# Full-width weights for the narrow value passes: zero columns in the coefficient tiles, and one more key block split, in a two-layer decoder trunk

## The chip, the cores and the metric

The kernel is one program on one core of a Trainium2 chip. The metric is device microseconds for one execution, as the median of the runs of a kernel. The engines are named as in the profile: PE is TensorE's matrix multiply, PEld its weight load, DVE is VectorE, ACT is ScalarE, POOL is GpSimd, SP is SyncE, which issues the large loads.

## The reference

256 tokens of width 1024 go through two layers. Each layer mixes tokens (an mLSTM in the first, an RG-LRU in the second, cross attention beside both), normalises, and then sends every token through 8 heads of 16 experts out of 16384 (PEER). The change lies in that last step:

```python
def block(xb):                       # for the tokens of one group
    q = (xb @ w_q).reshape(n, PEER_HEADS, 2, PEER_HALF)
    s = einsum('nhpc,pkc->nhpk', q, sk)
    sv, si = lax.top_k(s, PEER_TOPK)
    cand = sv[:, :, 0, :, None] + sv[:, :, 1, None, :]
    ...
    fv, fi = lax.top_k(cand, PEER_TOPK)
    gw = softmax(fv)
    act = gelu(einsum('nhkd,nd->nhk', u_tab[eid], xb))
    return einsum('nhk,nhkd->nd', gw * act, v_tab[eid])
...
x = layer_norm(DN_ALPHA * x + mix, ln1_g[i], ln1_b[i])
y = peer_ffn(x, peer_w_q[i], peer_subkeys[i], peer_u[i], peer_v[i])
x = layer_norm(DN_ALPHA * x + y, ln2_g[i], ln2_b[i])
```

Everything is float32.

## The kernel before

A layer runs in stages, one after the other: input projection, token mixer and cross attention, output projection, normalisation, PEER. Products of float32 matrices are mostly made of two parts each: a value is rounded to a shorter format (the high part, `H`), and what is left over is the low part (`L`); high by high, high by low and low by high are added up in PSUM.

PEER does not gather experts for the first 192 tokens. It treats the 16384 experts as 128 blocks of 128 and multiplies all of them:

- **Key stage.** For each key block, `u_step` (L1276) forms 128 experts by 192 tokens. A block is split into `wH` and `wL` and takes 8 pairs of matmuls (L1289, L1290), and one matmul later, the fold (L1299), which adds the tokens' low part; or it is "plain": the raw float32 block is multiplied in 8 calls of `fp32` (L306), which the trace shows as 16 matmuls, and nothing is split. `way` (L53) says which: of the first ten blocks, 3 and 7 are plain and the others are `POOLED`, that is, GpSimd makes their low part; some of the later ones are plain, the others are split on ACT and DVE. Beside this stage VectorE picks the top experts of each token (L1109 to L1117, with the scores `s` from L306), and then the dense gates.
- **Value stage.** For each of the 128 value blocks, the raw block is cast to `wH` on ACT (L146), the low part `wL` is `raw - wH` on DVE (L161), and the coefficients of the block go into a tile `cc`, 128 experts by 512 columns: ACT copies the 192 tokens' high part (L1524) and once more that of tokens 128 to 191 (L1525), DVE subtracts the low part (L1526). `coef` does this two blocks ahead.
- **The last 64 tokens** have their experts gathered row by row (POOL L1226), with a dot product (DVE L1246) and a weighted sum (DVE L1250) for each row. `deal` hands these out between the blocks, at rates from a table.

PE's work for one value block is ten matmuls of 512 streamed columns, weights from `cc`, streams from `wH` and `wL`: two at L1543 (`second`: low and high parts of tokens 128 to 191, 64 columns each, against `wH`, for each half of the model width), then L1552, L1553, L1552, L1553 and twice L1550 (`first`: tokens 0 to 127, high by high, low by high, high by low), then two at L1541 (`second` with `low`: high part of tokens 128 to 191 against `wL`). The last one has only 64 columns of weights, and only 64 partitions of its bank are written:

```python
mm(y[2 + k][:N - P], cc[:, P:N], l[:, ks], start=False, stop=False, ...)
```

Of `cc`, columns 0 to 191 hold the high parts of all tokens, 192 to 383 the low parts, and 384 to 447 again the high parts of tokens 128 to 191; 448 to 511 are not used. The tiles rotate through a pool of three buffers. In the first layer the last 3 blocks, in the second the last 7, are kept, and what is left of their passes comes after the loop in another order; the second layer has tiles of its own for their coefficients.

What sets the order: each engine runs its instructions in the order of the program. `pump` and `load` (L123 to L181) issue the load of a raw block on SP as soon as one of five raw buffers comes free; there are three buffers for `wH` and `wL`. `self.pool_cols` says how many columns of a low part go to GpSimd and how many to VectorE for a block of kind `None`; it is set to 1024 after the first half of the query projection and to 0 in `route`.

Of the kernel before, what the change touches and what calls it, by code (L numbers as in the profile page):

```python
# [7 lines left out]
F32 = mybir.dt.float32  # L8
F32R = mybir.dt.float32r
# [9 lines left out]
P = 128  # L19
# [34 lines left out]
def way(i):  # L54
    if i >= P - 1:
        return PLAIN
    if i >= N0:
        return PLAIN if i - N0 < STEPS and (i - N0) % 12 not in (1, 4, 6, 9, 11) else None
    if i < 10:
        return PLAIN if i % 4 == 3 else POOLED  # L60
    if i < 15:
        return PLAIN
    return PLAIN if i < 44 and i % 5 in (1, 3) else None
# [24 lines left out]
class Trunk:  # L88
# [1239 lines left out]
    def peer_layer(self, layer):  # L1328
        nc, tc, A = self.nc, self.tc, self.A
        self.layer = layer  # L1330
        with ExitStack() as ctx:
# [29 lines left out]
            with ExitStack() as rctx:  # L1361
# [23 lines left out]
                def route():  # L1385
                    for q in range(2):
                        self.score(qT, sk, ss[1], 1, q)
                    yield 0.1
                    yield from self.keys16(w, 1, ss[1], range(2))
                    for q in range(2):  # L1390
                        self.score(qT, sk, ss[0], 0, q)
                    yield from self.keys16(w, 1, ss[1], range(2, 4))
                    rest = self.keys16(w, 0, ss[0], range(4))
                    for c in rest:
                        yield c
                        if self.n_got >= self.u0[layer] + 2:
                            break
                    while self.n_got < self.u0[layer] + 2:
                        yield None
                    for q in range(2, 4):  # L1400
                        self.score(qT, sk, ss[1], 1, q)
                    for _ in range(2):
                        c = next(rest, None)
                        if c:
                            yield c
                    self.pool_cols = 0
                    yield from self.keys16(w, 1, ss[1], range(4, 8))
                    for q in range(2, 4):
                        self.score(qT, sk, ss[0], 0, q)
                    yield from self.routing(w, 1)  # L1410
                    first, n = self.ready, 0
                    for side in (rest, self.keys16(w, 0, ss[0], range(4, 8)), self.routing(w, 0)):
                        for c in side:
                            yield c
                            n += 1
                            if n == LATE:
                                first()
                                self.listed = True
                                yield 2.2
                    for _ in range(LATE):  # L1420
                        yield None
                    self.ready()
# [35 lines left out]
                for gq in range(2):  # L1458
                    qb = self.proj_t(8, (self.xH, self.xL))
                    for b in range(4):  # L1460
                        o = 8 * gq + 2 * b
                        put = (nc.scalar.copy, nc.vector.tensor_copy)[b % 2]
                        put(qT[:, o:o + 2, :].rearrange("p a b -> p (a b)"), qb[b])
                    if gq == 0:
                        def wait():
                            self.pool_cols = D
                            yield
                            yield from paced()
                        self.beside(wait())
# [47 lines left out]
            kept = HL_BUFS - 1  # L1517
            block = lambda i: lo[:, i, :] if i < N0 else hi[:, i - N0, :]

            kept, ccs = KEPT[layer], []  # L1520

            def coef(i):
                cc = ccs[i - P] if layer and i >= P - kept else cp.tile([P, 512], F32R, name="cc")
                nc.scalar.copy(cc[:, :N], block(i))  # L1524
                nc.scalar.copy(cc[:, 2 * N:3 * N - P], block(i)[:, P:])  # L1525
                nc.vector.tensor_sub(cc[:, N:2 * N], block(i), cc[:, :N].bitcast(F32))  # L1526
                return cc
            cs = [coef(0), coef(1)]
            g.append((self.u_step(), None))
# [7 lines left out]
            def second(part, k, low=False):  # L1537
                ks = slice(512 * k, 512 * k + 512)
                for i_, (h, l), cc in part:
                    if low:  # L1540
                        mm(y[2 + k][:N - P], cc[:, P:N], l[:, ks], start=False, stop=False, skip_group_check=True)  # L1541
                    else:
                        mm(y[2 + k], cc[:, N + P:N + 2 * P], h[:, ks], start=i_ == 0, stop=False, skip_group_check=True)  # L1543

            def first(part, c0, n, low=False):
                k, cs_ = c0 // 512, slice(c0, c0 + n)
                out = y[k][:, c0 - 512 * k:c0 - 512 * k + n]
                for i_, (h, l), cc in part:
                    if low:
                        mm(out, cc[:, :P], l[:, cs_], start=False, stop=False, skip_group_check=True)  # L1550
                    else:
                        mm(out, cc[:, :P], h[:, cs_], start=i_ == 0, stop=False, skip_group_check=True)  # L1552
                        mm(out, cc[:, N:N + P], h[:, cs_], start=False, stop=False, skip_group_check=True)  # L1553

            def lead(i):
                return min(HL_BUFS + max(0, min(kept - HL_BUFS, (i - RISE) // 3)), P - i)
            for i in range(P):
                late.append((i, self.next(lead(i)), cs.pop(0)))
                if layer and i == N0:
                    lo_p.close()  # L1560
                    t = right.enter_context(tc.tile_pool(name="tail1", bufs=1, side="right"))
                    self.extra = [[t.tile([P, D], F32R, name=f"v{z}{c}") for z in "HL"] for c in range(kept - HL_BUFS)]
                    ccs += [t.tile([P, 512], F32R, name=f"cc{c}") for c in range(kept)]
                    t.tile([P, 8], F32, name="gap")
                if i + 2 == CLOSES[layer]:
                    for _ in few:
                        pass
                    nc.sync.dma_start(last[1][P - NS:], last[0][:NS])
                    if layer == 0:
                        right.close()  # L1570
                        kv = self.later.enter_context(tc.tile_pool(name="kv1", bufs=1, side="right"))
                        self.memctx = self.later.enter_context(ExitStack())
                        m = self.memctx.enter_context(tc.tile_pool(name="mem1", bufs=1, side="right"))
                        self.wb = kv.tile([P, 28, P], F32, name="wb")
                        self.mem_dest(kv, m)
                        self.lncol = m.tile([P, 5, 2, DT], F32, name="lncol")[:, 0]
                        nc.sync.dma_start(self.lncol, A["ln_col"])
                        self.kvw = [(m.tile([P, D], F32R, name=f"kH{c}"), m.tile([P, D], F32R, name=f"kL{c}"))
                                    for c in range(3)]
                        self.part_v = m.tile([P, 512], F32, name="half")  # L1580
                if i + 2 < P:
                    cs.append(coef(i + 2))
                if layer == 0 and i == MEM1[0]:
                    nc.sync.dma_start(self.part_v, self.half_v)
                if i > 1:
                    self.deal(few, RATES[3][layer])
                if 0 <= i - JOIN[layer] < 4:
                    z, k = divmod(i - JOIN[layer], 2)
                    rs, ks = slice(P - NS, P), slice(512 * k, 512 * k + 512)
                    xs = x[rs, 1, ks]  # L1590
                    nc.vector.scalar_tensor_tensor(xs, xs, 1.0 if z else ALPHA, last[z][rs, ks], op0=ALU.mult, op1=ALU.add)
                if i < P - HALVED[layer]:
                    second(late[-1:], 0), second(late[-1:], 1)
                    first(late[-1:], 0, 512)
                    if i < P - kept:
                        first(late[-1:], 512, 512)
                        first(late[-1:], 512, 512, True)
                    first(late[-1:], 0, 512, True)
                    second(late[-1:], 0, True), second(late[-1:], 1, True)
                    if i < P - kept:  # L1600
                        late.pop()
# [24 lines left out]
            for low in (False, True):  # L1626
                for i_, (h, l), cc in late:
# [2 lines left out]
                        mm(out, cc[:, :P], l[:, ks], start=False, stop=False, skip_group_check=True)  # L1630
                    else:
                        mm(out, cc[:, :P], h[:, ks], start=i_ == late[0][0], stop=False, skip_group_check=True)
                        mm(out, cc[:, N:N + P], h[:, ks], start=False, stop=False, skip_group_check=True)
            if layer:
                for _ in self.norm(y, True, False):
                    pass
# [161 lines left out]
```

## Time and profile before

| | us |
|---|---|
| median of 3 runs | 1627.72 (1627.47 to 1627.94) |
| the profiled execution | 1626.55 |
| its span, first to last instruction | 1624.8 |
| PE busy in the span | 1610.8 (99%) |
| DVE busy | 1444.5 (89%) |
| ACT busy | 1012.3 (62%) |
| POOL busy | 519.5 (32%) |
| value stage of layer 0, first matmul | at 531.81 |
| value stage of layer 1, first matmul | at 1321.63 |

The granted clock of PE is 0.998 in the mean. A row of a timeline gives the start of a matmul, its duration, the line, the tiles, the size of its weights and its output. Matmuls are pipelined: a row's duration of some 390 ns is longer than the distance to the next row's start, so what a matmul costs is read from the distances between starts and not from durations.

### The profile page before, as it was taken

What the parts mean: (1) busy time and instruction counts of PE and PEld (TensorE: products, weight loads), DVE (VectorE), ACT (ScalarE), POOL (GpSimd) and SP (SyncE); (2) the same over time, 40 slices, a digit from 0 to 9 for tenths busy, and PEclk for the clock granted to TensorE, in tenths of its full rate; (3) what the DMA queues carried; (4) which work ended last, traced back from release to release, by engine and by line L of the source; (5) the groups of instructions that cost most, each with busy time, mean ns of one, the idle gap of its engine ahead of it and who ended that gap; (6) DMA issues with size and microseconds to landing.
All of it is one profiled execution on the core that took longest, in us unless ns stands there. A gap on an engine that the chain in (4) does not pass through costs nothing. (4 is left out here: it accounts for less than half of the span.)

```text
span 1624.8 us, 29358 instructions
## 1 busy us (share of the span) xinstructions
PE 1610.8 (99%) x10175; PEld 1454.6 (90%) x10175; DVE 1444.5 (89%) x2921; ACT 1012.3 (62%) x2281; POOL 519.5 (32%) x369
## 2 busy tenths in 40 slices
PE   9999999999999999999999999999999999999998
PEld 9999999999999777777789799999999987777776
DVE  6677899989999899998879989999999988989987
ACT  6554444567776666666768544445787766666664
POOL 3005623443224334331100164245222333343300
PEclk9999999999999999999999999999999999999999
DMA  7656759998889999999756375999888899999983
GB/s 254 210 178 227 245 208 332 334 349 296 288 298 356 335 356 361 351 352 302 269 201 201 100 260 195 327 308 365 313 283 298 315 346 352 345 354 343 351 289 135
DMA packets 133924, 470.42 MB, mean 290 GB/s; under 512 B 15116, under 2 KB 18960, under 8 KB 133520
## 3 DMA queue, kind: packets, MB, share of 16 engines
q1 hardware_dynamic: 94984, 330.64, 58.3%
q0 software_dynamic: 36864, 134.23, 22.6%
q10 hardware_dynamic: 1928, 3.67, 0.6%
q8 instruction: 81, 1.33, 0.3%
q14 instruction: 67, 0.55, 0.1%
HBM read 465.47 MB, written 1.31 MB: 287 GB/s over the span
## 5 line engine op out<-in xcount | busy, mean ns | idle before, releaser
L146 ACT CAST wH<-raw 128x1024 fp32r<-128x1024 f32 (+3 forms) x488 | 501.0, 1028 | 326.4 <-PE bank L1553 173.4
L161 DVE TENSOR_TENSOR wL<-raw,wH 128x1024 fp32r<-128x1024 f32 (+3 forms) x452 | 540.3, 1197 | 105.5 <-ACT wH L146 90.2
L1289 PE MATMUL bank<-xHL,wH 128*128 128x384 f32 x1280 | 378.7, 362 | 0.0
L1290 PE MATMUL bank<-xHL,wL 128*128 128x192 f32 x1280 | 320.3, 250 | 0.0
L1226 POOL DMA_INDIRECT row<-in_v_dram,lot x128 | 211.9, 1656 | 337.7 <-DVE rep L1250 292.4
L1226 POOL DMA_INDIRECT row<-in_u_rows_dram,lot x128 | 177.7, 1388 | 356.4 <-DVE sums L1246 183.7
L306 PE MATMUL bank<-xF,raw 128*128 128x192 f32 x1536 | 267.2, 328 | 0.0
L306 PEld LDWEIGHTS bank<-xF,raw 128*128 128x128 f32 x1536 | 247.4, 190 | 0.0
L1290 PEld LDWEIGHTS bank<-xHL,wL 128*128 128x128 f32 x1280 | 244.4, 191 | 0.0
L1289 PEld LDWEIGHTS bank<-xHL,wH 128*128 128x128 f32 x1280 | 240.5, 188 | 0.0
L1552 PE MATMUL bank<-wH,cc 128*128 128x512 f32 x488 | 192.5, 395 | 0.0
L1553 PE MATMUL bank<-wH,cc 128*128 128x512 f32 x488 | 190.1, 390 | 0.0
L1250 DVE SCALAR_TENSOR_TENSOR rep<-row,coefs,rep 128x1024 f32<-128x1024 f32 x124 | 158.4, 1278 | 0.0
L1246 DVE CUSTOM_DVE_ANT_0 row<-row,rep 128x1024 f32<-128x1024 f32 x128 | 155.9, 1218 | 0.4 <-DMA row<-in_u_rows_dram,lot 0.2
L1541 PE MATMUL bank<-wL,cc 128*64 128x512 f32 x488 | 153.1, 394 | 0.0
L1543 PE MATMUL bank<-wH,cc 128*128 128x512 f32 x488 | 151.5, 391 | 0.0
L1550 PE MATMUL bank<-wL,cc 128*128 128x512 f32 x488 | 149.8, 387 | 0.0
L159 POOL TENSOR_TENSOR wL<-raw,wH 128x1024 fp32r<-128x1024 f32 (+1 forms) x46 | 95.3, 2076 | 141.1 <-DVE x L355 87.4
L235 PE MATMUL bank<-xHL,wL 128*128 128x256 f32 x488 | 136.2, 279 | 1.3 <-POOL wL L151 0.6
L233 PE MATMUL bank<-xHL,wH 128*128 128x256 f32 x488 | 136.9, 280 | 0.4 <-ACT xHL L498 0.4
L234 PE MATMUL bank<-xHL,wH 128*128 128x256 f32 x488 | 135.7, 278 | 0.9 <-DVE xHL L502 0.7
L1274 ACT ACTIVATE oh<-oh,gL 128x128 f16<-128x128 f16 x384 | 125.8, 434 | 8.3 <-DVE oh L1268 8.2
(379 smaller groups left out, 2733.0 us busy)
## 6 DMA issues: line engine op xcount, KB each, us to landing
raw<-in_v_dram SPq DMA_DIRECT2D x256, 512.0 KB
raw<-in_u_dram SPq DMA_DIRECT2D x242, 512.0 KB
raw<-in_w_q_dram SPq DMA_DIRECT2D x32, 512.0 KB
raw<-in_w_out_dram SPq DMA_DIRECT2D x16, 512.0 KB
wglo<-in_u_dram SPq DMA_DIRECT2D x14, 512.0 KB
raw<-in_w0qx_dram SPq DMA_DIRECT2D x8, 512.0 KB
raw<-in_w0v_dram SPq DMA_DIRECT2D x8, 384.0 KB
raw<-in_w0o_dram SPq DMA_DIRECT2D x8, 384.0 KB
```

The source lines that it names most:

```text
L146: (nc.vector.tensor_copy if self.cast_dve else nc.scalar.copy)(h[:, c], r[:, c])
L161: rest = lambda l=l, r=r, h=h, c=slice(k, n): nc.vector.tensor_sub(l[:, c], r[:, c], h[:, c].bitcast(F32))
L306: self.nc.tensor.matmul(out, lhsT, rhs, start=start, stop=stop, skip_group_check=True)
L1226: self.nc.gpsimd.indirect_dma_start(to, None, rows, bass.IndirectOffsetOnAxis(ap=self.lot[:, 0, n:n + 1].bitcast(I32), axis=0))
L1246: nc.vector.tensor_tensor_reduce(r, r, rep, 1.0, 0.0, ALU.mult, ALU.add, sums[:, n:n + 1])
L1250: nc.vector.scalar_tensor_tensor(acc[0] if n == NS - 1 else rep, r, c, rep, op0=ALU.mult, op1=ALU.add)
L1289: mm(two(g[:, :2 * N]), h[:, c], two(self.xHL[:, dt, :])[:, :, :N], start=dt == 0, stop=False, skip_group_check=True)
L1290: mm(g[:, :N], l[:, c], self.xH[:, dt, :N], start=False, stop=False, skip_group_check=True)
L1541: mm(y[2 + k][:N - P], cc[:, P:N], l[:, ks], start=False, stop=False, skip_group_check=True)
L1543: mm(y[2 + k], cc[:, N + P:N + 2 * P], h[:, ks], start=i_ == 0, stop=False, skip_group_check=True)
L1552: mm(out, cc[:, :P], h[:, cs_], start=i_ == 0, stop=False, skip_group_check=True)
L1553: mm(out, cc[:, N:N + P], h[:, cs_], start=False, stop=False, skip_group_check=True)
```

## The change

The diff does four things.

1. Of the first ten key blocks of each layer, block 3 is no longer plain. It is of kind `None`: cast on ACT (L146), low part on VectorE (L161), two-part matmuls and a fold. Block 7 stays plain.
2. `self.pool_cols = 0` moves from `route` to the end of the second half of the query projection, which comes earlier.
3. The coefficient tiles are three fixed tiles, taken in turn, in place of a pool that rotates. Columns 192 to 255 of each are set to zero once, by a multiplication of 64 columns of the identity by 0 (`blank`); the seven tiles of the second layer's last blocks are treated likewise when they are made, at value block 64. The low part of the coefficients moves from column 192 to column 256, the second copy of the high part from 384 to 448.
4. The last pass of each block (L1541 before, L1548 after) has 128 columns of weights, 64 of coefficients and 64 of zeros, and writes all 128 partitions of its bank; to the lower half it adds zeros.

```diff
-        return PLAIN if i % 4 == 3 else POOLED
+        return {3: None, 7: PLAIN}.get(i, POOLED)
...
-                    self.pool_cols = 0
...
-                    if gq == 0:
+                    if gq:
+                        self.pool_cols = 0
+                    else:
...
-            kept, ccs = KEPT[layer], []
+            kept, LOW = KEPT[layer], 2 * P
+
+            def blank(cc):
+                nc.vector.tensor_scalar(cc[:, N:LOW], self.ident[:, :LOW - N], 0.0, None, op0=ALU.mult)
+                return cc
+            ring = [blank(cp.tile([P, 512], F32R, name=f"cc{k}", bufs=1)) for k in range(HL_BUFS)]
+            ccs = {}
...
-                cc = ccs[i - P] if layer and i >= P - kept else cp.tile([P, 512], F32R, name="cc")
+                cc = ccs.get(i, ring[i % HL_BUFS])
                 nc.scalar.copy(cc[:, :N], block(i))
-                nc.scalar.copy(cc[:, 2 * N:3 * N - P], block(i)[:, P:])
-                nc.vector.tensor_sub(cc[:, N:2 * N], block(i), cc[:, :N].bitcast(F32))
+                nc.scalar.copy(cc[:, LOW + N:], block(i)[:, P:])
+                nc.vector.tensor_sub(cc[:, LOW:LOW + N], block(i), cc[:, :N].bitcast(F32))
...
-                        mm(y[2 + k][:N - P], cc[:, P:N], l[:, ks], start=False, stop=False, skip_group_check=True)
+                        mm(y[2 + k], cc[:, P:LOW], l[:, ks], start=False, stop=False, skip_group_check=True)
                     else:
-                        mm(y[2 + k], cc[:, N + P:N + 2 * P], h[:, ks], start=i_ == 0, stop=False, skip_group_check=True)
+                        mm(y[2 + k], cc[:, LOW + P:], h[:, ks], start=i_ == 0, stop=False, skip_group_check=True)
...
-                        mm(out, cc[:, N:N + P], h[:, cs_], start=False, stop=False, skip_group_check=True)
+                        mm(out, cc[:, LOW:LOW + P], h[:, cs_], start=False, stop=False, skip_group_check=True)
...
-                    ccs += [t.tile([P, 512], F32R, name=f"cc{c}") for c in range(kept)]
+                    for c in range(kept):
+                        ccs[P - kept + c] = blank(t.tile([P, 512], F32R, name=f"late{c}"))
```

Three places show what this does to the order of the instructions.

PE, in the middle of layer 0's value stage, one block before the change (`cc` is the coefficient tile, the sizes are those of the output):

```order
L1543 MATMUL bank<-wH,cc 128x512 x2
L1552 MATMUL bank<-wH,cc 128x512
L1553 MATMUL bank<-wH,cc 128x512
L1552 MATMUL bank<-wH,cc 128x512
L1553 MATMUL bank<-wH,cc 128x512
L1550 MATMUL bank<-wL,cc 128x512 x2
L1541 MATMUL bank<-wL,cc 64x512 x2
```

and one after it (`cc_6537` is one of the three fixed tiles):

```order
L1550 MATMUL bank<-wH,cc_6537 128x512 x2
L1559 MATMUL bank<-wH,cc_6537 128x512
L1560 MATMUL bank<-wH,cc_6537 128x512
L1559 MATMUL bank<-wH,cc_6537 128x512
L1560 MATMUL bank<-wH,cc_6537 128x512
L1557 MATMUL bank<-wL,cc_6537 128x512 x2
L1548 MATMUL bank<-wL,cc_6537 128x512 x2
```

The ten matmuls stand in the same order; the last two write 128 partitions in place of 64, and the line numbers are 7 higher.

DVE, at the start of layer 0's value stage (`wglo` and `wghi` are the coefficients of the first and second half of the blocks; L1524 after is `blank`, L1533 after the low part of L1526 before), a piece of the difference:

```order
 L161 TENSOR_TENSOR wL<-raw,wH 128x1024
 L1326 TENSOR_TENSOR wghi<-wghi,bank 128x192
-L1526 TENSOR_TENSOR cc<-wglo,cc 128x192 x2
+L1524 TENSOR_SCALAR cc_6537<-ident 128x64
+L1524 TENSOR_SCALAR cc_6539<-ident 128x64
+L1524 TENSOR_SCALAR cc_6541<-ident 128x64
+L1533 TENSOR_TENSOR cc_6537<-wglo,cc_6537 128x192
+L1533 TENSOR_TENSOR cc_6539<-wglo,cc_6539 128x192
 L161 TENSOR_TENSOR wL<-raw,wH 128x1024
```

Three operations of 64 columns come ahead of the coefficients of the first two blocks; everything else keeps its place.

DVE, early in layer 0's key stage, after the query projection (`s` are the scores, `sv` and `sidx` the top values and their places, `qT` the queries):

```order
 L1111 MAX_INDEX sidx_1659<-sv_1657,s_1663 128x8 x2
 L1113 MATCH_REPLACE tmp<-sv_1657,s_1663 128x128 x2
-L1463 COPY qT<-bank 128x512 x2
+L1462 COPY qT<-bank 128x512 x2
 L1115 MAX sv_1657<-tmp 128x8 x2
 L1117 MAX_INDEX sidx_1659<-sv_1657,tmp 128x8 x2
+L161 TENSOR_TENSOR wL<-raw,wH 128x1024
 L1109 MAX sv_1658<-s_1664 128x8 x2
 L1111 MAX_INDEX sidx_1660<-sv_1658,s_1664 128x8 x2
```

The low part of key block 3 is one more VectorE operation, just ahead of the first maximum of the next scores. On ACT the cast of this block and the copy for its fold are added; on PE its 8 plain matmuls give way to pairs of L1289 and L1290, with the fold after the next block has begun. In layer 1 the same happens at the same places, and seven more `blank` operations stand at value block 64. POOL and SP issue the same instructions in the same order.

More of the change, by code (lines that the diff above doesn't have):

```diff
@@ L1632, in peer_layer @@
                         mm(out, cc[:, :P], h[:, ks], start=i_ == late[0][0], stop=False, skip_group_check=True)
-                        mm(out, cc[:, N:N + P], h[:, ks], start=False, stop=False, skip_group_check=True)
+                        mm(out, cc[:, LOW:LOW + P], h[:, ks], start=False, stop=False, skip_group_check=True)
             if layer:
```

## The prediction

> **What bounds the kernel now.** I read the page's busy line first, then the table of stretches, then PE's timeline in the value stage, then its groups by shape.
>
> ```profile
> PE 1610.8 (99%) x10175; PEld 1454.6 (90%) x10175; DVE 1444.5 (89%) x2921; ACT 1012.3 (62%) x2281; POOL 519.5 (32%) x369
> GB/s 254 210 178 227 245 208 332 334 349 296 288 298 356 335 356 361 351 352 302 269 201 201 100 260 195 327 308 365 313 283 298 315 346 352 345 354 343 351 289 135
> ```
>
> In the stretches, the first is in layer 0's key stage, the next in its value stage, the last in layer 1's value stage (columns: busy us of each engine, clock, share of the DMA engines, GB/s):
>
> ```profile
> core 0: us, PE busy (x) PEld busy (x) DVE busy (x) ACT busy (x) POOL busy (x), PEclk, DMA share, GB/s
> 187.00:346.00 159.00, 159.00 (x1090) 159.00 (x1090) 147.81 (x445) 80.30 (x161) 66.97 (x41) 1.00 0.84 298
> 640.00:720.00 80.00, 80.00 (x350) 61.61 (x349) 73.03 (x89) 50.60 (x106) 30.66 (x20) 1.00 0.97 359
> 1340.00:1420.00 80.00, 80.00 (x349) 61.66 (x349) 72.02 (x88) 50.71 (x106) 30.87 (x19) 1.00 0.96 350
> ```
>
> PE is busy in all 80.00 us of the value stretches, at full granted clock, and no wait stands in it. So only what changes PE's own time per block counts, as long as DVE (73.03 of 80) and the DMA engines (0.97) keep up. One block of the value stage, from L1541 to the next L1541:
>
> ```profile
> 577.37 0.63 PE L1541 MATMUL bank<-wL,cc 128*64 128x512 f32 x2
> 577.83 0.62 PE L1543 MATMUL bank<-wH,cc 128*128 128x512 f32 x2
> 578.29 0.40 PE L1552 MATMUL bank<-wH,cc 128*128 128x512 f32 x1
> 578.52 0.39 PE L1553 MATMUL bank<-wH,cc 128*128 128x512 f32 x1
> 578.75 0.40 PE L1552 MATMUL bank<-wH,cc 128*128 128x512 f32 x1
> 578.98 0.39 PE L1553 MATMUL bank<-wH,cc 128*128 128x512 f32 x1
> 579.21 0.61 PE L1550 MATMUL bank<-wL,cc 128*128 128x512 f32 x2
> 579.67 0.63 PE L1541 MATMUL bank<-wL,cc 128*64 128x512 f32 x2
> ```
>
> Starts are 0.46 us apart for two matmuls, whatever the line: ten take 579.67 − 577.37 = 2.30 us, 230.0 ns each. The two with 64 columns are neither shorter nor longer than the others.
>
> **The value stage: the rhythm of PE.** Is 230.0 ns all that such a matmul can do? Two stretches say no. The first is the end of layer 1's value stage, where the kept blocks' passes are grouped by kind: six with 64 columns, then eighteen with 128, on the same coefficient and value tiles. The second is layer 0's output projection, all with 128 columns.
>
> ```profile
> 1606.11 0.40 PE L1541 MATMUL bank<-wL,cc 128*64 128x512 f32 x1
> ...
> 1607.49 0.39 PE L1552 MATMUL bank<-wH,cc 128*128 128x512 f32 x1
> ...
> 1611.57 0.28 PE L1552 MATMUL bank<-vH,cc 128*128 128x256 f32 x1
> ```
>
> ```profile
> 120.54 0.39 PE L233 MATMUL bank<-eH,mixH 128*128 128x512 f32 x1
> ```
>
> ```profile
> 127.80 0.39 PE L235 MATMUL bank<-wH,mixL 128*128 128x512 f32 x1
> ```
>
> Six with 64 columns take 1607.49 − 1606.11 = 1.38 us, 230 ns each. The eighteen behind them take 1611.57 − 1607.49 = 4.08 us, 226.7 each. The 32 of the projection take 127.80 − 120.54 = 7.26 us, 226.9 each. So a 512-column matmul goes at 226.7 ns in a stretch that has only full-width weights, and at 230.0 in one that mixes in, or consists of, 64-column weights. A block with two narrow weights in ten never comes to the faster rhythm: that is how I read the 3.3 ns, and it is the assumption on which this prediction rests.
>
> After the change all ten have 128 columns. Per block 10 × (230.0 − 226.7) = 33 ns, period 2.267 us. The loop has 128 − 3 = 125 whole blocks in layer 0 and 128 − 7 = 121 in layer 1: 246 × 33 ns = **8.1 us**. The kept blocks' grouped passes are few (six narrow ones at 1606.11 would save 6 × 3.3 = 20 ns): nothing.
>
> The price of the wider weights is in PE's groups, weight loads apart:
>
> ```profile
> L1541 PEld LDWEIGHTS bank<-wL,cc 128*64 128x64 f32 x488 | 65.6, 134 | 31.8
> L1543 PEld LDWEIGHTS bank<-wH,cc 128*128 128x128 f32 x488 | 91.3, 187 | 34.8 <-issue 0.4
> ```
>
> A load grows from 134 to 187 ns. It costs nothing so long as a load lies beside the matmul ahead of it: 187 is less than 226.7, and eight of ten passes hide such a load today. The Trainium skill ("TensorE: Matmul & The Clock Gate", LDWEIGHTS) speaks against this change: load time is the number of columns over 1.2, by estimate 53 ns for 64 and 107 for 128. The trace agrees on the difference (53) and not on the height (134 and 187). Taken as a cost on the path it would make the sum 512 × 53 ns = 27 us worse (two loads in each of 256 blocks); by the rows, where full-width passes are spaced like narrow ones, it is zero.
>
> **The cover in the value stage.** A block of 2.267 us asks 2.300/2.267 = 1.015 times the rate of everything. DVE's 73.03 of 80 us becomes 74.1, 93%. ACT is at 50.60. The DMA share of 0.97 becomes 0.98, at 359 × 1.015 = 364 GB/s; one slice of the page shows 365. That is the tightest point and gets a rival below.
>
> **The blanks.** The trace has no such operation. The nearest row is the subtraction of 192 columns:
>
> ```profile
> L1526 DVE TENSOR_TENSOR cc<-wglo,cc 128x192 fp32r<-128x192 f32 x128 | 44.8, 351 | 0.0
> ```
>
> 64 columns of one operand are below it: between 0 and 351 ns, I take 200. At a value stage's start three stand ahead of the first two coefficient subtractions:
>
> ```profile
> 528.44 0.62 DVE L1526 TENSOR_TENSOR cc<-wglo,cc 128x192 fp32r<-128x192 f32 x2
> ```
>
> ```profile
> 531.81 0.65 PE L1543 MATMUL bank<-wH,cc 128*128 128x512 f32 x2
> ```
>
> The subtractions end at 529.06, PE needs them at 531.81: 2.75 us of cover against 3 × 0.351 = 1.05 at most. Queued behind are the low part of a value block and three gate products, late by the same; PE takes up the value block two blocks later, the gate products 64 blocks later. In layer 1 seven more stand at block 64, at most 2.5 us of DVE time in a stretch where it has (80 − 72.02)/80 = 10% free; coefficients are made two blocks ahead, 4.6 us. Zero, with a bound of 1 us if that cover is thinner than I think. The fixed tiles in place of rotating ones: three buffers either way, zero.
>
> **Key block 3.** Plain and split blocks follow each other here (the matmuls of L1299 are folds):
>
> ```profile
> 195.02 0.28 PE L1299 MATMUL bank<-low,ident 128*128 128x192 f32 x1
> 195.13 2.78 PE L306 MATMUL bank<-xF,raw 128*128 128x192 f32 x16
> 197.62 0.39 PE L1299 MATMUL bank<-low,ident 128*128 128x192 f32 x1
> 197.84 0.36 PE L1289 MATMUL bank<-xHL,wH 128*128 128x384 f32 x1
> ...
> 200.13 1.97 PE L306 MATMUL bank<-sk,qT 128*128 128x128 f32 x16
> ```
>
> The plain block with the fold behind it runs from 195.13 to 197.84, 2.71 us. The split one takes 200.13 − 197.84 = 2.29, and two folds at 195.13 − 195.02 = 0.11 each: 2.51. Gain 0.2 us a layer, **0.4 us** in all. For it DVE takes on a low part and ACT a cast:
>
> ```profile
> L161 DVE TENSOR_TENSOR wL<-raw,wH 128x1024 fp32r<-128x1024 f32 x398 | 486.7, 1224 | 84.4 <-ACT wH L146 69.2 <-issue 12.3 <-ACT cc L1524 1.8
> 190.27 0.49 DVE L1109 MAX8 sv<-s 128x8 f32<-128x128 f32 x2 [2.19 <-ACT s L1128]
> ```
>
> The low part (1.22 us) stands ahead of the maximum that today comes after 2.19 us of idling for ACT's scores, so that idle time covers most of it; queued behind is the routing, whose gates PE uses only after 64 key blocks. ACT is busy 80.30 of 159. If the low part came late PE would wait, at most its 1.22 us a layer: bounds of −0.4 and +2.4 us, and I take −0.4. Moving the `pool_cols` line makes this block's low part VectorE's; POOL and SP issue what they did.
>
> **The sum.** The profiled execution took 1626.55 us, 1.2 below the median of the runs and outside their interval, with a span of 1624.8. −8.1 − 0.4 = −8.5: 1618.1 for it, and 1627.72 − 8.5 = **1619.2 us** for the median.
>
> **The rivals.** 0.2%, 3.3 us, is what I count as a difference.
>
> *A. The rhythm stays at 230.0 (0.15).* The narrow weights need not be what keeps PE from 226.7: a block also changes value tile, coefficient tile and bank. Against it: the projection at 120.54 changes value tiles too and holds 226.9, and the six narrow passes at 1606.11 are at 230 in one bank. For it: both fast stretches are short. Then only the key blocks' gain is left: 1627.3.
>
> *B. Part of the gain (0.10).* Either the DMA engines, at 0.98, deliver late in some stretches, or PE falls into the fast rhythm only in some blocks. Half of the gain: 4.1 + 0.4, 1623.2. The 365 GB/s lasted one slice of 41 us; a value stage lasts 128 × 2.3 = 294.
>
> *C. A slower rhythm (0.08).* Full-width weights are no warrant of 226.7. In layer 1's output projection, all with 128 columns:
>
> ```profile
> 912.32 0.39 PE L233 MATMUL bank<-wH,mixH 128*128 128x512 f32 x1
> ...
> 913.72 0.39 PE L233 MATMUL bank<-wH,mixH 128*128 128x512 f32 x1
> ```
>
> six matmuls take 1.40 us, 233.3 each. Should the value loop with its moved columns settle there, each block takes 2.333: 246 × 33 = 8.1 us more, 1627.7 + 8.1 − 0.4 = 1635.4. It decides from the first whole block on; it becomes slower as soon as the mean distance is above 230.2. Against it: the eighteen at 1607.49 use the same kinds of tiles and run at 226.7, but with the low part still at column 192.
>
> *D. The wider loads show (0.01).* 512 × 53 ns: 1654. Against it stand the eight passes in ten that hide 187 ns today.
>
> *E. A switch of weight shape stalls PE (0.02).* Were each change from 128 columns to 64 and back to cost a drained pipe, then two in each block would go, at most 0.39 − 0.23 = 0.16 us each (a row's duration less the distance): 246 × 0.32 = 79 us, 1548. The block's rows speak against it: 577.37 and 577.83, where the shape changes, follow at the common 0.46 per pair. The Trainium skill ("TensorEngine Tiling (Array Packing)", Key Properties) says that changing the tiling mode drains TensorE; if a narrow weight is such a mode, the trace shows no drain of it.
>
> **How the numbers follow.** The forecast has 0.64. Its own range: 226.0 to 227.3 for the rhythm is 246 × 40 to 246 × 27 ns, 9.8 to 6.6 us, and key and blank costs from −0.4 to +2: 1617.5 to 1623. For 8 in 10 the range must reach to B and A, and it then leaves out C, D and E (0.11): low 1617.0 (with 0.5 us between runs), high 1627.7 (A with its small costs). Faster: the forecast, E and two thirds of B, 0.64 + 0.02 + 0.07 = 0.73. Same: A and the rest of B, 0.18. Slower: C and D, 0.09.
>
> **What would show it.** Right: in the value stage starts of the same line 2.267 us apart, all ten some 227 ns, no wait of PE that names DMA, `wL` or `cc`; weight loads of the last pair at 187 ns; value stages shorter by 125 × 33 ns = 4.1 us and 4.0 us; key block 3 as 8 pairs and a fold, 0.2 us shorter. Wrong: a period of 2.300 (A) or 2.333 (C), or a period that varies with PE idle for the raw block's landing (B); a wait of PE at the key block behind block 3; a late first matmul of the value stage.

## The result, and the profile after

| | before | after |
|---|---|---|
| median, us | 1627.41 (1626.65 to 1627.94, 6 runs) | 1618.07 (1617.85 to 1619.29, 6 runs) |
| ratio | | 0.9944, 95% interval 0.9931 to 0.9957 |
| the profiled execution | 1626.55 | 1618.03 |
| its span | 1624.8 | 1616.2 |
| value stage of layer 0 starts | 531.81 | 531.24 |
| value stage of layer 1 starts | 1321.63 | 1317.07 |

The kernel became 9.3 us faster in the median, 8.5 us between the two profiled executions. The busy line of the page after, and the same three stretches as before the change:

```profile
PE 1602.7 (99%) x10177; PEld 1482.1 (92%) x10177; DVE 1446.4 (89%) x2936; ACT 1013.4 (63%) x2285; POOL 522.1 (32%) x369
```

```profile
core 0: us, PE busy (x) PEld busy (x) DVE busy (x) ACT busy (x) POOL busy (x), PEclk, DMA share, GB/s
187.00:346.00 159.00, 159.00 (x1093) 159.00 (x1092) 148.18 (x444) 81.36 (x163) 66.89 (x40) 1.00 0.84 298
640.00:720.00 80.00, 80.00 (x355) 66.26 (x354) 73.98 (x90) 51.48 (x108) 31.05 (x19) 1.00 0.98 359
1340.00:1420.00 80.00, 80.00 (x354) 66.27 (x353) 72.89 (x90) 51.39 (x108) 30.29 (x18) 1.00 0.97 354
```

PE has shed 8.1 us of busy time and is as full as before. DVE rose from 73.03 to 73.98 in the second stretch, the DMA share from 0.97 to 0.98; neither has made PE wait. One block after the change, on PE's timeline (L1548 is the pass that was L1541):

```profile
578.45 0.61 PE L1548 MATMUL bank<-wL,cc 128*128 128x512 f32 x2
578.90 0.62 PE L1550 MATMUL bank<-wH,cc 128*128 128x512 f32 x2
579.35 0.39 PE L1559 MATMUL bank<-wH,cc 128*128 128x512 f32 x1
579.58 0.39 PE L1560 MATMUL bank<-wH,cc 128*128 128x512 f32 x1
579.81 0.39 PE L1559 MATMUL bank<-wH,cc 128*128 128x512 f32 x1
580.03 0.39 PE L1560 MATMUL bank<-wH,cc 128*128 128x512 f32 x1
580.26 0.62 PE L1557 MATMUL bank<-wL,cc 128*128 128x512 f32 x2
580.71 0.39 PE L1548 MATMUL bank<-wL,cc 128*128 128x512 f32 x1
```

From 578.45 to 580.71 are 2.26 us where 2.30 stood. Over 100 blocks it can be read more finely:

```profile
576.63 0.62 PE L1550 MATMUL bank<-wH,cc 128*128 128x512 f32 x2
...
803.30 0.61 PE L1550 MATMUL bank<-wH,cc 128*128 128x512 f32 x2
```

803.30 − 576.63 = 226.67 us, a period of 2.267 us. The weight load of this pass is now as long as the others, and the blanks at the start of layer 0's value stage are short:

```profile
L1548 PEld LDWEIGHTS bank<-wL,cc 128*128 128x128 f32 x482 | 90.5, 188 | 18.7
```

```profile
527.86 0.40 DVE L1524 TENSOR_SCALAR cc<-ident 128x64 fp32r<-128x64 f32 x3
528.17 0.62 DVE L1533 TENSOR_TENSOR cc<-wglo,cc 128x192 fp32r<-128x192 f32 x2
```

```profile
531.24 0.65 PE L1550 MATMUL bank<-wH,cc 128*128 128x512 f32 x2
```

The three blanks put the subtractions back by 528.17 − 527.86 = 0.31 us; PE's first matmul still comes 2.45 us behind their end (528.79). The seven of layer 1, from 1464.06 on, took 0.91 us and made nobody wait.

Key block 3 of layer 0, between the fold of block 1 and the score products that follow block 4 (each L1299 is a fold):

```profile
194.65 0.28 PE L1299 MATMUL bank<-low,ident 128*128 128x192 f32 x1
...
199.45 0.28 PE L1299 MATMUL bank<-low,ident 128*128 128x192 f32 x1
199.56 1.97 PE L306 MATMUL bank<-sk,qT 128*128 128x128 f32 x16
```

It takes 199.56 − 194.65 = 4.91 us against 200.13 − 195.02 = 5.11 before: 0.20 less. DVE makes the new low part in what was idle time, and PE waits for nothing:

```profile
189.40 1.23 DVE L161 TENSOR_TENSOR wL<-raw,wH 128x1024 fp32r<-128x1024 f32 x1 [1.69 <-ACT wH L146]
```

The profiled difference adds up. The value loops give 246 × 33.3 ns = 8.2 us and the two key blocks 0.4, together the 8.6 by which the spans differ. The rest is small wandering with both signs: the fold at 194.65, which on PE stands ahead of the split block, was already 0.37 us earlier than the same fold before the change, at 195.02, and about as much is lost again before layer 1's value stage starts.

### The profile page after: what moved, and what is told of

Its sections match the earlier page's. It is cut to its first block, busy times and chain, and to the rows that moved or that the text cites. A ratio compares the mean times of both kernels' runs of the same rounds, so it can differ in the third digit from the quotient of the medians.

```text
span 1616.2 us, 29381 instructions
## 1 busy us (share of the span) xinstructions
PE 1602.7 (99%) x10177; PEld 1482.1 (92%) x10177; DVE 1446.4 (89%) x2936; ACT 1013.4 (63%) x2285; POOL 522.1 (32%) x369
## 5 line engine op out<-in xcount | busy, mean ns | idle before, releaser
L146 ACT CAST wH<-raw 128x1024 fp32r<-128x1024 f32 (+3 forms) x490 | 503.4, 1029 | 327.0 <-PE bank L1560 172.3
L161 DVE TENSOR_TENSOR wL<-raw,wH 128x1024 fp32r<-128x1024 f32 (+3 forms) x454 | 542.7, 1197 | 97.5 <-ACT wH L146 93.6
L1289 PE MATMUL bank<-xHL,wH 128*128 128x384 f32 x1296 | 383.3, 362 | 0.0
L1290 PE MATMUL bank<-xHL,wL 128*128 128x192 f32 x1296 | 324.3, 250 | 0.0
L306 PE MATMUL bank<-xF,raw 128*128 128x192 f32 x1504 | 261.6, 328 | 0.0
L1290 PEld LDWEIGHTS bank<-xHL,wL 128*128 128x128 f32 x1296 | 247.4, 191 | 0.0
L1289 PEld LDWEIGHTS bank<-xHL,wH 128*128 128x128 f32 x1296 | 243.5, 188 | 0.0
L306 PEld LDWEIGHTS bank<-xF,raw 128*128 128x128 f32 x1504 | 242.3, 190 | 0.0
L1560 PE MATMUL bank<-wH,cc 128*128 128x512 f32 x482 | 187.1, 388 | 0.0
L1559 PE MATMUL bank<-wH,cc 128*128 128x512 f32 x482 | 187.1, 388 | 0.0
L1250 DVE SCALAR_TENSOR_TENSOR rep<-row,coefs,rep 128x1024 f32<-128x1024 f32 x124 | 158.7, 1280 | 0.0
L1550 PE MATMUL bank<-wH,cc 128*128 128x512 f32 x482 | 148.7, 389 | 0.0
L1548 PE MATMUL bank<-wL,cc 128*128 128x512 f32 x482 | 148.4, 389 | 0.0
L1557 PE MATMUL bank<-wL,cc 128*128 128x512 f32 x482 | 148.1, 388 | 0.0
```

The lines of the kernel that those rows point to most:

```text
L146: (nc.vector.tensor_copy if self.cast_dve else nc.scalar.copy)(h[:, c], r[:, c])
L161: rest = lambda l=l, r=r, h=h, c=slice(k, n): nc.vector.tensor_sub(l[:, c], r[:, c], h[:, c].bitcast(F32))
L306: self.nc.tensor.matmul(out, lhsT, rhs, start=start, stop=stop, skip_group_check=True)
L1250: nc.vector.scalar_tensor_tensor(acc[0] if n == NS - 1 else rep, r, c, rep, op0=ALU.mult, op1=ALU.add)
L1289: mm(two(g[:, :2 * N]), h[:, c], two(self.xHL[:, dt, :])[:, :, :N], start=dt == 0, stop=False, skip_group_check=True)
L1290: mm(g[:, :N], l[:, c], self.xH[:, dt, :N], start=False, stop=False, skip_group_check=True)
```

## The experiments

Theory 1 is the prediction's: 64-column weights keep PE out of the 226.7 ns rhythm. Theory 2 is that moving the columns of the coefficient tile does it, with the zeros beside the point; rival C, a slow rhythm that comes from where the tiles lie, is of the same family. Each run is one kernel. Block periods come from rows 100 blocks apart (80 in e2); times of runs with a single execution are good to some 1.5 us (the kernel before itself ran between 1625.59 and 1628.28 beside them), the periods to 0.001.

| run | weights of the last two passes | coefficient tiles against the changed kernel's | period, us | time, us (kernel before beside it) |
|---|---|---|---|---|
| before | 64 | old columns | 2.300 | 1627.41 |
| after | 128 | as changed | 2.267 | 1618.07 |
| e1 | 64 | as changed | 2.300 | 1625.80 (1626.52) |
| e2 | 128 | old columns | 2.267 | 1619.22 (1626.52) |
| e4 | one 64, one 128 | as changed | 2.287 | 1623.51 (1626.52) |
| e5 | 96 | as changed | 2.313 | 1629.82 (1627.90) |
| e8 | 64, and all others 64 | as changed | 2.300 | 1626.15 (1627.90) |
| e10 | 128 | 64 bytes lower | 2.289 | 1623.13 (1627.26) |
| e9 | 128 | 128 bytes lower | 2.324 | 1632.74 (1627.26) |
| e6 | 128 | 192 bytes lower | 2.333 | 1633.53 (1627.90) |
| e11 | 64 | old columns, 192 bytes lower | 2.327 | 1632.40 (1627.26) |

**e1: the narrow weights put back.**

```diff
-mm(y[2 + k], cc[:, P:LOW], l[:, ks], ...)
+mm(y[2 + k][:N - P], cc[:, P:N], l[:, ks], ...)
```

> The changed kernel with the last two passes of each value block at 64 columns of weights again (and 64 partitions of output); columns moved, zero columns and key block 3 as changed. Theory 1 (the narrow weights keep PE from the 226.7 ns rhythm): block period 2.300 us, time about 1618.1 + 8.1 = 1626.2 us. Theory 2 (the place of the coefficients' columns in the tile does it): period 2.267 us, time 1618.1 us.

Rows 100 blocks apart:

```profile
577.20 0.62 PE L1550 MATMUL bank<-wH,cc 128*128 128x512 f32 x2
...
807.20 0.62 PE L1550 MATMUL bank<-wH,cc 128*128 128x512 f32 x2
```

230.00 us: 2.300 a block, with the columns moved and the zeros written. Ratio to the kernel before 0.9996 (0.9986 to 1.0006). Theory 2 falls.

**e2: full width alone, in the old tile.** The other 64 partitions of the bank then get the product of neighbouring columns in place of zeros; PE's work is that of the changed kernel.

```diff
-mm(y[2 + k][:N - P], cc[:, P:N], l[:, ks], ...)
+mm(y[2 + k], cc[:, P:2 * P], l[:, ks], ...)
```

> The kernel before with one edit: the last two passes of each value block take 128 columns of weights, columns 128 to 255 of the old tile, so that the low parts of tokens 0 to 63 stand where the zeros would be and add their (small, wrong) product to the low partitions; no column moved, no blanks, rotating tiles, key block 3 plain. Theory 1 (narrow weights): period 2.267 us, time 1627.4 - 8.1 = 1619.3 us. Theory 2 (place of the columns): period 2.300 us, time 1627.4 us.

Rows 80 blocks apart:

```profile
576.64 0.61 PE L1543 MATMUL bank<-wH,cc 128*128 128x512 f32 x2
```

```profile
757.97 0.61 PE L1543 MATMUL bank<-wH,cc 128*128 128x512 f32 x2
```

181.33 / 80 = 2.267. Ratio 0.9955 (0.9939 to 0.9972): nearly all of the gain from that one line. With e1 this shows theory 1's cause, in both directions. Near the end of layer 0's loop, at 798 us, this kernel lost 0.6 us around one wait for a cast on ACT, which the changed one did not.

**e3: key block 3 alone.** The edit is the first two parts of the diff on the kernel before.

> The kernel before with key block 3 split and the earlier setting of the column count alone. Forecast's reading: key block 3 with both folds 2.51 us in place of 2.71, in each layer, no wait of PE behind it; start of layer 0's value stage 0.2 us earlier from this cause, value period 2.300 us, time about 0.4 us below the kernel before. Rival: the low part comes late and PE waits up to 1.2 us at the block in a layer: 0.4 us lower to 2.4 us higher.

The folds around the two blocks:

```profile
194.69 0.28 PE L1299 MATMUL bank<-low,ident 128*128 128x192 f32 x1
...
199.49 0.28 PE L1299 MATMUL bank<-low,ident 128*128 128x192 f32 x1
```

From the first to the last it is 4.80 us, as in the changed kernel, and no wait of PE stands behind the block. The single time, 1626.38 beside 1626.52, agrees with 0.4 but could not prove it; the trace does for the block.

**e4: one narrow pass a block.**

```diff
+w, c = (P, LOW) if k else (N - P, N)
-mm(y[2 + k], cc[:, P:LOW], l[:, ks], ...)
+mm(y[2 + k][:w], cc[:, P:c], l[:, ks], ...)
```

> The changed kernel with only the first of the two last passes of a value block at 64 columns, the second at 128. If each narrow pass costs its own share, 16.5 ns: period 2.283 us, time about 1622.2 us. If one narrow weight per block is enough to keep the whole block out of the fast rhythm: 2.297 to 2.300 us, about 1626 us. If one alone does no harm: 2.267 us, 1618.1 us.

A block of it, from the narrow L1549 to the next narrow one:

```profile
602.90 0.62 PE L1549 MATMUL bank<-wL,cc 128*64 128x512 f32 x2
603.37 0.63 PE L1551 MATMUL bank<-wH,cc 128*128 128x512 f32 x2
603.83 0.39 PE L1560 MATMUL bank<-wH,cc 128*128 128x512 f32 x1
...
605.19 0.40 PE L1549 MATMUL bank<-wL,cc 128*64 128x512 f32 x1
```

The four distances from 602.90 to 603.83 average 232.5 ns, the six from there to 605.19 226.7. So a narrow weight disturbs itself and three full ones behind it, 20 to 25 ns in all, and then PE is back in its rhythm; none of the three expected outcomes had this form, though 2.287 is nearest to the first. Two narrow ones in a row cost 33 ns and, as the kernel before shows, leave no fast stretch long enough to see.

**e5: 96 columns.** `cc[:, P:P + 96]` into `y[2 + k][:96]`.

> The changed kernel with the last two passes of each value block at 96 columns of weights and 96 partitions of output. If whatever is short of 128 breaks the rhythm alike: period 2.300 us, about 1626 us. If the loss goes with the missing columns: half, 2.283 us, about 1622 us. If 96 is wide enough: 2.267 us, 1618 us.

```profile
577.89 0.40 PE L1548 MATMUL bank<-wL,cc 128*96 128x512 f32 x1
```

```profile
809.22 0.40 PE L1548 MATMUL bank<-wL,cc 128*96 128x512 f32 x1
```

231.33 us for 100 blocks: 2.313, slower than with 64. No expectation had that. The loss does not go with the missing columns; the padding pays only in full.

**e8: all passes narrow.** Every pass of the value loop takes the first 64 columns of its weights from the second block on.

> The changed kernel with every pass of the value loop at 64 columns of weights from the second block on (left out: tokens 64 to 127 of the first product and the second half of the columns in the second one). If the mixture of widths breaks the rhythm and a pure stream of narrow ones is steady: period 2.267 us, about 1618 us. If a narrow weight is slower by itself, as the six at the end of the kernel before suggest (230 ns): 2.300 us, about 1626 us.

```profile
578.34 0.63 PE L1551 MATMUL bank<-wH,cc 128*64 128x512 f32 x2
```

```profile
808.34 0.61 PE L1551 MATMUL bank<-wH,cc 128*64 128x512 f32 x2
```

230.00 us, a period of 2.300: a pure stream of narrow weights is at 230 ns too. It takes no mixture of widths to lose the fast rhythm; narrow weights alone do it at this place. (The other columns' products are left out, so this run speaks of the rhythm alone.)

**e6, e9, e10: the place of the tiles.** A spacer stands ahead of the coefficient tiles. Its width, 56 columns, is set to 8, 24 and 40, which lowers the tiles by 192, 128 and 64 bytes and changes nothing else.

```diff
-GAP, GAP_R = 56, 8
+GAP, GAP_R = 8, 8
```

> The changed kernel with the spacer ahead of the coefficient tiles 8 columns wide in place of 56, so that all coefficient tiles lie 192 bytes lower against the value tiles; nothing else differs. Rival C (the place of the tiles chooses the rhythm, and the slow one of layer 1's output projection is among them): period 2.333 us, about 1618.1 + 246 x 0.066 = 1634 us. Theory 1 (width alone): period 2.267 us, 1618.1 us.

> The changed kernel with the spacer at 24 columns: coefficient tiles 128 bytes lower against the value tiles than in the changed kernel. If only equal places are fast: 2.333 us as with 192 bytes, about 1634 us. If the rhythm is graded with the place: between 2.267 and 2.333, some 1618 to 1634. If another place is faster still: below 2.267 us, below 1618 us.

> The changed kernel with the spacer at 40 columns: coefficient tiles 64 bytes lower than in the changed kernel. The same three outcomes: 2.333 us and about 1634 us if only equal places are fast; between, if graded; below 2.267 us if this place is better.

Rows of e6, 100 blocks apart:

```profile
577.67 0.63 PE L1550 MATMUL bank<-wH,cc 128*128 128x512 f32 x2
```

```profile
811.01 0.63 PE L1550 MATMUL bank<-wH,cc 128*128 128x512 f32 x2
```

of e9:

```profile
578.66 0.63 PE L1550 MATMUL bank<-wH,cc 128*128 128x512 f32 x2
```

```profile
811.04 0.62 PE L1550 MATMUL bank<-wH,cc 128*128 128x512 f32 x2
```

and of e10:

```profile
576.60 0.62 PE L1550 MATMUL bank<-wH,cc 128*128 128x512 f32 x2
```

```profile
805.49 0.62 PE L1550 MATMUL bank<-wH,cc 128*128 128x512 f32 x2
```

233.34, 232.38 and 228.89 us: 2.333, 2.324, 2.289. The same instructions with the same full-width weights run at 226.7 to 233.3 ns, graded with the place: e6 came out at rival C's figure, e9 and e10 at the graded outcome. By the program's layout the value tiles and all coefficient columns of the changed kernel start at equal addresses modulo 256 bytes. So do those of e2, where the low part lies at 768 bytes in its tile and the second product's weights at 1280: three and five times 256, and as fast. The rhythm that rival C borrowed from layer 1's output projection is real, and a spacer of another width would have made it this change's result.

The spacer moves the weights and leaves the streams where they are, so these runs alone do not say whether the weights' own address counts or their place against the stream. Layer 1's output projection in the changed kernel tells the two apart. Its weights `mixH` and `mixL` stay in one place, modulo 256; the first streams, `eH` and `eL`, start at the same place as the weights, and the later ones, `wH` and `wL`, 192 bytes above it:

```profile
904.40 0.39 PE L235 MATMUL bank<-eH,mixL 128*128 128x512 f32 x1
...
905.76 0.39 PE L235 MATMUL bank<-eH,mixL 128*128 128x512 f32 x1
```

```profile
908.13 0.39 PE L233 MATMUL bank<-wH,mixH 128*128 128x512 f32 x1
...
909.76 0.40 PE L234 MATMUL bank<-wL,mixH 128*128 128x512 f32 x1
```

Six distances in 1.36 us are 226.7 ns each at the equal place, seven in 1.63 are 232.9 with the weights 192 bytes lower, as in e6. It is the place against the stream that counts. Layer 0's output projection, the prediction's fast stretch, has equal places throughout.

**e11: narrow weights at the slow place.** The kernel before with the spacer at 8.

> The kernel before, narrow weights and all, with the spacer at 8 columns: coefficient tiles 192 bytes lower, the place at which the changed kernel runs at 2.333 us. If narrow weights cost on top of the place: above 2.333 us, over 1635.6 us. If the narrow weights restart the rhythm at every block and the place matters less for them: between 2.300 and 2.333 us, 1627.4 to 1635.6 us; the change would then gain nothing at this place or lose up to 8 us.

```profile
577.83 0.63 PE L1543 MATMUL bank<-wH,cc 128*128 128x512 f32 x2
```

```profile
810.50 0.63 PE L1543 MATMUL bank<-wH,cc 128*128 128x512 f32 x2
```

232.67: 2.327, between the two, as the second expectation had it. Compared with e6 (2.333), full-width weights at this place cost 7 ns a block, 246 × 7 = 1.7 us, where at the place of the changed kernel they gain 33 ns. By the periods, the sign of the change hangs on the place; the two times, 1632.40 and 1633.53, are too close for single executions.

**e7: how near is the next bound?** The last two passes are left out of the loop.

> The changed kernel without the last two passes of each value block inside the loop (left out: high part of tokens 128 to 191 by the low part of the values), so that PE needs 8 x 226.7 ns = 1.81 us a block. It asks how near the next bound is. If the DMA share of 0.98 means what it says: period 2.22 to 2.27 us, no or little gain, 1606 to 1618 us, PE waiting for wH or wL behind landings. If DVE is next (73.98 of 80 us): 2.10 us, about 1577 us. If neither: 1.81 us, about 1507 us.

1591.16 us, 26.9 below the changed kernel, 0.11 us a block. Two stretches and PE's main wait:

```profile
560.00:600.00 40.00, 38.08 (x157) 28.23 (x155) 40.00 (x51) 27.88 (x58) 32.83 (x12) 1.00 1.01 396
680.00:720.00 40.00, 38.04 (x157) 28.15 (x156) 40.00 (x51) 28.20 (x60) 33.05 (x11) 1.00 1.02 397
```

```profile
PE bank L1550 <- DVE cc L1533: 31.3, 22, 7.7
```

In these stretches DVE is busy in all 40 us, and 157 matmuls, eight a block, take 40 us: 2.04 us a block, 0.23 less than in the changed kernel. There DVE sets the pace. The DMA engines moved 396 GB/s where 359 had read as a share of 0.98. So the share near 1 was no bound, and rival B's reason falls.

The 31.3 us that PE waited for coefficients are not all DVE's work, though. DVE itself stood still three times, for gathered rows of the last 64 tokens:

```profile
DVE rep L1250 <- DMA row<-in_v_dram,lot: 20.3, 3, 7.0
```

```profile
741.87 1.28 DVE L1250 SCALAR_TENSOR_TENSOR rep<-row,coefs,rep 128x1024 f32<-128x1024 f32 x1 [7.03 <-DMA row<-in_v_dram,lot]
```

```profile
744.70 1.19 PE L1550 MATMUL bank<-wH,cc 128*128 128x512 f32 x2 [7.66 <-DVE cc L1533]
```

PE's longest wait follows one of these directly. So two things come next behind PE: DVE's own work, and now and then the landing of a gathered row. The 0.11 us a block is what the run gained under both, not DVE's distance alone.

**e12: another stream at an equal place.** Two small constant tiles are allocated ahead of `xHL`, which puts it at an equal address to `wH` and `wL` modulo 256; in the changed kernel it lies 64 bytes off.

```diff
+self.c8 = c.tile([P, 6], F32, name="c8")
+self.n8 = c.tile([P, 6], F32, name="n8")
 self.xHL = c.tile([P, DT, 2 * T], F32R, name="xHL")
```

> The changed kernel with two small constant tiles (c8, n8) allocated ahead of the token tile xHL in place of behind it: xHL, streamed in the key stage, the projections and the query products, lies 64 bytes higher, at a whole multiple of 256 bytes from wH and wL, as the coefficient tiles of the value stage do; every other tile but x and cp, which move along, stays. Does the rule of places hold for other shapes? If equal places are fast for every shape: the pairs L1289 and L1290 come below 287 ns, and the time falls below 1618 us by 1.3 us for each ns. If the place matters for 512-column streams alone: 287 ns, 1618.1 us. If the 256-column streams go the other way, as those at the end of the value stage suggest (120 ns at an equal place, 113.3 in the query projection at an unequal one): the projections get slower, 488 x 3 x 6.7 ns = 9.8 us, 1627.9 us with unchanged pairs.

The query projection of layer 0, here:

```profile
150.05 0.28 PE L233 MATMUL bank<-xHL,wH 128*128 128x256 f32 x1
...
152.33 0.28 PE L234 MATMUL bank<-xHL,wH 128*128 128x256 f32 x1
```

and in the changed kernel:

```profile
149.99 0.28 PE L233 MATMUL bank<-xHL,wH 128*128 128x256 f32 x1
...
152.37 0.28 PE L233 MATMUL bank<-xHL,wH 128*128 128x256 f32 x1
```

19 distances in 2.28 us are 120.0 ns, 21 in 2.38 are 113.3. The pairs of the key stage hardly moved, from 285.8 to 286.9 ns in the mean. The kernel took 1625.62 us (ratio to the kernel before 0.9992, 0.9983 to 1.0002), 7.5 above the changed kernel's median, which was not taken again beside it. By the spans of the two profiled executions (1624.4 and 1616.2) the loss is 8.2 us: 6.5 ahead of the key stages, where 9.8 had been expected, and 1.7 in them. Why the projections lost less than their distances say was not followed up. For 256-column streams the equal place is the slow one; the third expectation came nearest, and the rule of e6 does not carry over as it stands. No run that does the whole work came below the changed kernel.

## Why the prediction was right

- **The value stage's sum** held: 246 blocks at 33.3 ns, 8.2 us against 8.1. The reading on which it rested, that narrow weights keep PE from 226.7 ns, is shown by e1 and e2 in both directions. It was not the whole condition: full width gives 226.7 only where weights and stream lie at equal places, which the prediction did not know.
- **The key block** held: 0.20 us in layer 0, by its rows and by e3, with no wait for the low part.
- **What was to stay hidden** stayed hidden. The blanks took 0.10 us each where 0.2 was assumed, and lie beside other work. The wider loads, 188 ns, show nowhere: the passes with the longest loads are the faster ones (rival D).
- **Rival A** fell to e1 and e2, **rival E** to e4: a block that switches from 128 columns to 64 and back loses some 20 ns in all, nothing like two drains of 160.
- **Rival B** did not come about, and its reason was weak: a DMA share of 0.98 at 359 GB/s was no ceiling, as 396 in e7 shows. That step put a limit on the wrong resource; in the full stretches of e7 DVE, which was held to be free enough at 93%, sets the pace, and three waits for gathered rows show in PE's time.
- **Rival C** was the best-founded danger and had only 0.08. Its mechanism is shown (e6, e9); what kept it away was the place of the tiles, which the changed columns preserve modulo 256 bytes. The prediction argued from the eighteen matmuls at 1607.49, which lie at equal places too, without knowing that this was the reason. That the new columns kept the place was luck.
- **Size.** The median moved 9.3 us against 8.5 forecast; the two profiled executions differ by 8.5. The rest lies within what the runs of each kernel spread.

What stays open is why a narrow weight, or a place, changes the distance. In the records a load of 128 columns starts with the matmul ahead of it; that the two readers, of the weights and of the stream, meet in memory is a guess that no run tests.

## What to carry to other kernels

Read what a matmul costs from distances between starts, and compare the same shape in several stretches of one kernel: a gap of 3 ns is a gain of 8 us when it stands in 2,500 rows. Before padding weights, find a stretch that already runs at full width with the same tiles in the same place; here padding to 96 lengthened the block, from 2.300 to 2.313 us, and padding at another address did too, from 2.327 to 2.333. After any change of tile sizes ahead of a hot loop, look at the loop's rhythm again.

## What the runs showed of the hardware

- Matmuls with 512 streamed columns and 128 columns of weights stood 226.7, 228.9, 232.4 or 233.3 ns apart in the mean, with the weights 0, 64, 128 or 192 bytes lower than their stream, modulo 256 (the changed kernel, e10, e9, e6). With 256 streamed columns it was 113.3 ns with the weights 64 bytes above the stream (the changed kernel) and 120.0 at equal places (e12).
- The Trainium skill ("TensorE: Matmul & The Clock Gate", Step-by-step: what each phase is for) says that loading the next weights takes no read bandwidth from the running matmul, since the two have ports of their own. If that is taken to mean that the place of the weights cannot slow the stream, the measurement decides against it: in e6 and the changed kernel the instructions are equal, only the weights' place is not, and the distance grows by 6.7 ns. Whether it is read bandwidth that is lost, no run shows.
- Loads took 134, 161 and 188 ns for 64, 96 and 128 columns (the kernel before, e5, the changed kernel), 27 ns for each 32. The Trainium skill's rule ("TensorE: Matmul & The Clock Gate", LDWEIGHTS), columns over 1.2, has that slope; the runs add a constant of some 80 ns, hidden here beside the matmul ahead, since 188 is less than 226.7.
